# Sums of weight quarters in the first feed-forward product: additions on VectorE, or accumulating transfers issued by GpSimd

## The chip, the core and the metric

The kernel runs on one core of a Trainium2 chip. The metric is the device time of one execution in microseconds (us). Five engines run their own instruction streams in order and wait for one another through semaphores: TensorE (PE, matmuls), VectorE (DVE), ScalarE (ACT), GpSimd (POOL) and SyncE (SP, which here only issues transfers). Transfers (DMA) are carried by 16 DMA engines, whichever engine issued them.

## The reference

One layer of a hybrid encoder, in float32, for 512 tokens of width 2048: a mixer (a gated short convolution and a gated linear attention), its output projection, and a feed-forward block. The change lies in the first product of the feed-forward block, `h @ w_ff1[l]`, of 512 x 2048 by 2048 x 8192.

```python
x = x + y @ w_out[l]
h = rmsnorm(x, norm2_g[l])
x = x + jnp.square(jax.nn.relu(h @ w_ff1[l])) @ w_ff2[l]
return rmsnorm(x, norm_f_g)
```

## The kernel before

Matmuls run on float32 values that are split in two: "hi" is the value cast to the matmul's own float type (ACT), "lo" is the rest, value minus hi (DVE). A product of two such operands is three matmuls, hi by hi, hi by lo and lo by hi.

The first feed-forward product goes through 32 groups (`for g in range(NPAIR)`), each for 256 of the 8192 columns. In a group the product is done block by block with seven block products instead of eight, a scheme of Strassen's kind. The weight has four quarters of 128 x 1024 numbers (512 KB), b11, b12, b21 and b22; the activations stand ready in seven combinations, `hforms`, computed before the loop. The seven products, called forms here, need these weights:

| form | weight | output bank | remark |
|---|---|---|---|
| 1 | b12 | f1a | copied out as q1 before form 2 adds to the bank |
| 2 | b22 | f1a | onto form 1 |
| 5 | b11 + b12 | f1c | copied out as q5 before form 3 adds to the bank |
| 3 | b21 | f1c | onto form 5 |
| 7 | b11 + b21 | f1d | |
| 6 | b11 + b12 + b21 | f1b | |
| 4 | b11 + b12 + b21 + b22 | f1e | |

Each form is 24 matmuls of 256 columns (8 steps by three) and takes its weight through `split_w`: a cast on ACT into one of three "hi" buffers, a subtraction on DVE into one of three "lo" buffers. The three buffers go round in program order, so a cast waits until PE has ended the form three places earlier in that order. Before, the order is 1, 5, 7, 3, 6, 2, 4. The sums come from `plus`, a DVE addition of two 128 x 1024 tiles into one of three "w" buffers, four a group. At the end DVE and ACT combine the banks into the tile y, ACT squares it, and 512 KB go to DRAM (`a_keep`), to be read by the second feed-forward product.

The quarters are loaded by SP into four "raw" buffers, which belong to a pool (`wp`) that serves the whole kernel. The pool `f1`, with the w tiles, y, q1, q5, u and v, is opened for this loop; its memory is that of the residual tiles `xr`, which are stored to DRAM (`x_keep`) just ahead of the loop. PSUM has eight banks "fb", of which a group takes five.

The kernel's text is recorded and ordered anew by a scheduler: on an engine instructions need not stand in the order of the text, though the order is fixed once built. Names in the rows below: `raw_f_21`, `w_f_20` are group 2's tiles of quarter 1 and 0 as they stand in `w_ff1` (0 is b12, 1 is b11, 2 is b21, 3 is b22), `hi_f_83` is group 8's hi of form 3, a last number is a buffer's.

Of the kernel before, what the change touches and what calls it, by code (L numbers as in the profile page):

```python
# [29 lines left out]
UNIT = 1056  # L30
HALF = SEQ // 2
NPAIR = D_FF // (2 * P)
FORMS = (1, 5, 7, 3, 6, 2, 4)
RAWS = 4
# [5 lines left out]
def hymba_kernel(  # L40
# [3 lines left out]
    nc = tc.nc  # L44
    V, S, T, G = nc.vector, nc.scalar, nc.tensor, nc.gpsimd
# [3 lines left out]
    wp = ctx.enter_context(tc.tile_pool(name="wp", bufs=2))  # L49
# [81 lines left out]
    for t, s in ((g2t, g2), (cgt, conv_g), (cwt, conv_w)):  # L131
# [13 lines left out]
        out=later, in_=later, pattern=[[-1, P]], compare_op=ALU.is_gt, fill=0.0,  # L145
# [45 lines left out]
    with tc.tile_pool(name="mix", bufs=1) as mix:  # L191
# [153 lines left out]
        for k in range(8):  # L345
            b = feature_major(w_feat[HEADS + k], u, f"og{k}")
            t = mix.tile([P, SEQ], F32, name=f"ogt_{k}", tag=f"hs{k % 2}")
# [3 lines left out]
        for h in range(HEADS):  # L351
            b = feature_major(w_feat[h], u, f"q{h}")
            q = mix.tile([P, SEQ], F32, name=f"q_{h}", tag=f"q{h}")
            V.scalar_tensor_tensor(
                out=q, in0=b, scalar=float(DK) ** -0.5, in1=r1b, op0=ALU.mult, op1=ALU.mult
# [127 lines left out]
    a_keep = tc.dram_tile([NPAIR, P, 2 * SEQ], F32, name="a_keep")  # L483
# [102 lines left out]
    def fbank(name):  # L586
        return fb.tile([P, 512], F32, name=name, tag="fb", bufs=8)


    with tc.tile_pool(name="f1", bufs=1, reuse_waits="tile") as f1:  # L590
        for g in range(NPAIR):
            raws = []
            for q in range(4):
                raw = wp.tile([P, UNIT], F32, name=f"raw_f1_{g}{q}", tag="raw", bufs=RAWS)
                nc.sync.dma_start(raw[:, :1024], w_ff1[4 * g + q])
                raws.append(raw[:, :1024])
            b12, b11, b21, b22 = raws

            def split_w(f, src):
                hi = wp.tile([P, UNIT], F32R, name=f"hi_f1_{g}{f}", tag="hi", bufs=3)  # L600
                lo = wp.tile([P, UNIT], F32R, name=f"lo_f1_{g}{f}", tag="lo", bufs=3)
                S.copy(hi[:, :1024], src)  # L602
                V.tensor_tensor(out=lo[:, :1024], in0=src, in1=hi[:, :1024].bitcast(F32), op=ALU.subtract)  # L603
                return hi, lo

            def plus(f, in0, in1):
                w = f1.tile([P, 1024], F32, name=f"w_{g}{f}", tag="w", bufs=3)
                V.tensor_tensor(out=w, in0=in0, in1=in1, op=ALU.add)  # L608
                return w

            def product(f, w, dst, start):
                hi, lo = split_w(f, w)
                for p in range(8):
                    c = slice(p * P, (p + 1) * P)
                    sh, sl = hforms[p][f]
                    for m, (l, r) in enumerate(((hi, sh), (hi, sl), (lo, sh))):
                        T.matmul(  # L617
                            dst[:, :HALF], l[:, c], r, start=start and p == m == 0,
                            stop=p == 7 and m == 2, skip_group_check=True,
                        )  # L620

            def half(name, bufs=2):
                return f1.tile([P, HALF], F32, name=f"{name}_{g}", tag=name, bufs=bufs)

            ba, bc, bd, bb, be = (fbank(f"f1{k}_{g}") for k in "acdbe")
            y = f1.tile([P, 2, SEQ], F32, name=f"y_{g}", tag="y", bufs=2)
            t1, t2 = slice(0, HALF), slice(HALF, SEQ)
            product(1, b12, ba, True)
            q1 = half("q1")
            S.copy(q1, ba[:, :HALF])  # L630
            w1 = plus(5, b11, b12)
            product(5, w1, bc, True)
            q5 = half("q5")
            S.copy(q5, bc[:, :HALF])
            product(7, plus(7, b11, b21), bd, True)
            product(3, b21, bc, False)
            w3 = plus(6, w1, b21)
            product(6, w3, bb, True)
            u_ = half("u")
            V.tensor_tensor(out=u_, in0=bb[:, :HALF], in1=q1, op=ALU.subtract)  # L640
            v_ = half("v")
            V.tensor_tensor(out=v_, in0=bd[:, :HALF], in1=u_, op=ALU.add)
            V.tensor_tensor(out=y[:, 0, t1], in0=bc[:, :HALF], in1=u_, op=ALU.add)
            V.tensor_tensor(out=y[:, 0, t2], in0=q5, in1=v_, op=ALU.add)
            product(2, b22, ba, False)
            product(4, plus(4, w3, b22), be, True)
            S.activation(y[:, 1, t1], ba[:, :HALF], AF.Relu)
            V.tensor_tensor(out=y[:, 1, t2], in0=be[:, :HALF], in1=v_, op=ALU.subtract)
            S.activation(y[:, 0, :], y[:, 0, :], AF.Relu)
            S.activation(y[:, 1, t2], y[:, 1, t2], AF.Relu)  # L650
            S.activation(y, y, AF.Square)
            nc.gpsimd.dma_start(a_keep[g], y.rearrange("p a b -> p (a b)"))

# [13 lines left out]
    with tc.tile_pool(name="ff", bufs=1, reuse_waits="tile") as ff:  # L667
# [19 lines left out]
        for blk in range(4):  # L687
            a = []
# [5 lines left out]
            for n in range(4):  # L694
                bs = [fbank(f"f2_{blk}{n}{i}") for i in range(NT)]
                for j in range(nu):
                    h, l = unit(w_ff2[(blk * 4 + n) * 8 + j], 1024, f"f2_{blk}{n}{j}")
                    for i in range(NT):
                        t = slice(i * P, (i + 1) * P)
# [8 lines left out]
        w2 = {}  # L708
        for n in range(4):
            for j in (6, 7):  # L710
                raw = wp.tile([P, UNIT], F32, name=f"raw_e{n}{j}", tag="raw", bufs=RAWS)
# [4 lines left out]
        for i in range(NT):  # L716
            t = slice(i * P, (i + 1) * P)
            x3 = x3s[i]
            for n in range(4):
                b = fbank(f"e_{i}{n}")  # L720
# [14 lines left out]
            for n in range(2):  # L735
# [3 lines left out]
                out=x3[:, cs[3]], in0=x3[:, cs[3]], scalar=r3, in1=gft[:, cs[3]], op0=ALU.mult, op1=ALU.mult  # L739
# [65 lines left out]
```

## Time and profile before

| | |
|---|---|
| median of 3 runs | 2172.0 us (2170.23 to 2172.83) |
| the profiled execution | 2173.21 us, its span 2171.3 us |
| granted TensorE clock, mean | 0.995 |
| busy: PE, DVE, ACT, POOL | 2137.6, 1141.4, 763.8, 29.1 us |
| DMA | 263.24 MB, 121 GB/s on average |
| the edited loop, first matmul to last store issued | 787.6 to 1438.9 us |

The span is from the first to the last instruction on the core. The page lists groups of equal instructions by line, engine and operation with what they write and read ("hi_f<-w"), their count, their busy time and the mean of one, and the idle time ahead of them with what ended it. The chain of waits follows the work that ended last. A timeline row gives start, duration, engine, line, operation, and in brackets the idle time before it with its releaser. A DMA row gives the issuing queue, the count, the size of one, and the median time from issue to landing. In rows cut from a window the releaser after "<-" is what the engine waited for.

### The profile page before, as it was taken

The page shows a single profiled execution, that of the slowest core. Times are in us where ns is not written, and L with a number is a line of the kernel's source. Part 1 is how long each engine was busy: PE and PEld are TensorE (multiplying, and loading weights), DVE is VectorE, ACT ScalarE, POOL GpSimd, SP SyncE. Part 2 cuts the span into 40 slices and gives each one's busy share as a digit, 9 for nine tenths or more (in the row PEclk, how much of TensorE's full clock was granted, in tenths as well). Part 3 has the DMA queues.
Part 4 walks back from the last instruction along what each step waited for, and adds up shares of the span by engine and source line. Part 5 has one row for each costly group of instructions (what it writes and reads, how often), then busy time and mean ns, then how long its engine had stood idle before and what let it go on. Part 6 is the DMA issues. An engine that isn't in the chain of part 4 may idle for free.

```text
span 2171.3 us, 28976 instructions
## 1 busy us (share of the span) xinstructions
PE 2137.6 (98%) x12248; PEld 1863.1 (86%) x12248; DVE 1141.4 (53%) x1336; ACT 763.8 (35%) x980; POOL 29.1 (1%) x60
## 2 busy tenths in 40 slices
PE   8999999999999989999999999989999999999998
PEld 6988877777888889999999999977888888888886
DVE  4232236656754487777777777745243233322345
ACT  6242212222333345545554554533122122121133
POOL 0000000000000000000000000000000000000000
PEclk9999999999999999999999999999999999999999
DMA  7222222222242243444334334466243343222232
GB/s 290 84 87 97 92 79 92 78 78 78 88 174 88 92 151 127 136 131 136 133 127 136 131 133 135 137 230 216 97 156 108 96 134 128 90 96 97 97 117 78
DMA packets 71090, 263.24 MB, mean 121 GB/s; under 512 B 8037, under 2 KB 8085, under 8 KB 68784
## 3 DMA queue, kind: packets, MB, share of 16 engines
q1 hardware_dynamic: 64224, 230.85, 32.2%
q0 software_dynamic: 6736, 30.55, 3.5%
q8 instruction: 95, 1.56, 0.3%
q14 instruction: 35, 0.29, 0.0%
HBM read 236.20 MB, written 25.17 MB: 120 GB/s over the span
## 4 chain that ended last, share of the span: by engine, by line
PE 88%; issue 8%; DMA 3%; DVE 1%; ACT 1%; SPq 0%; POOL 0%; ACTq 0%; POOLq 0%
PE f L75 10%; PE f L76 10%; PE f L77 10%; PE f1c L617 8%; PE f1a L617 8%; PE f1b L617 4%; PE f1d L617 4%; PE f1e L617 4%; DMA a<-a_keep 2%; PE fm_ch L75 1%; PE fm_cc L75 1%; PE tm_v L75 1%; PE tm_v L76 1%; PE tm_v L77 1%; PE fm_og L77 1%
## 5 line engine op out<-in xcount | busy, mean ns | idle before, releaser
L71 DVE TENSOR_TENSOR lo_f<-raw_f,hi_f 128x1024 fp32r<-128x1024 f32 x120 | 146.8, 1224 | 342.7 <-ACT hi_f L70 342.7
L70 ACT CAST hi_f<-raw_f 128x1024 fp32r<-128x1024 f32 x120 | 125.8, 1049 | 412.7 <-PE f L77 408.8
L603 DVE TENSOR_TENSOR lo_f<-w,hi_f 128x1024 fp32r<-128x1024 f32 x128 | 156.8, 1225 | 114.0 <-ACT hi_f L602 113.1
L602 ACT CAST hi_f<-w 128x1024 fp32r<-128x1024 f32 x128 | 134.6, 1051 | 160.5 <-PE f1c L617 107.7
L617 PE MATMUL f1c<-Sh,hi_f 128*128 128x256 f32 x512 | 145.0, 283 | 6.2 <-ACT hi_f L602 6.2
L617 PE MATMUL f1c<-Sh,lo_f 128*128 128x256 f32 x512 | 145.0, 283 | 0.4 <-DVE lo_f L603 0.4
L617 PE MATMUL f1c<-Sl,hi_f 128*128 128x256 f32 x512 | 144.7, 283 | 0.0
L617 PE MATMUL f1a<-Sh,hi_f 128*128 128x256 f32 x512 | 144.2, 282 | 0.0
L617 PE MATMUL f1a<-Sh,lo_f 128*128 128x256 f32 x512 | 144.1, 282 | 0.0
L617 PE MATMUL f1a<-Sl,hi_f 128*128 128x256 f32 x512 | 144.0, 281 | 0.0
L602 ACT CAST hi_f<-raw_f 128x1024 fp32r<-128x1024 f32 x96 | 100.9, 1051 | 110.2 <-PE f1b L617 55.7
L603 DVE TENSOR_TENSOR lo_f<-raw_f,hi_f 128x1024 fp32r<-128x1024 f32 x96 | 117.2, 1221 | 12.4 <-ACT hi_f L602 12.3
L75 PE MATMUL tm_op<-hi_op,yh 128*128 128x512 f32 (+1 forms) x304 | 106.2, 349 | 0.0
L76 PE MATMUL tm_op<-lo_op,yh 128*128 128x512 f32 (+1 forms) x304 | 105.3, 346 | 0.0
L77 PE MATMUL tm_op<-hi_op,yl 128*128 128x512 f32 (+1 forms) x304 | 105.0, 345 | 0.0
L617 PEld LDWEIGHTS f1c<-Sh,hi_f 128*128 128x128 f32 x512 | 97.6, 191 | 6.4 <-ACT hi_f L602 6.4
L617 PEld LDWEIGHTS f1c<-Sh,lo_f 128*128 128x128 f32 x512 | 97.4, 190 | 0.7 <-DVE lo_f L603 0.7
L617 PEld LDWEIGHTS f1c<-Sl,hi_f 128*128 128x128 f32 x512 | 97.2, 190 | 0.0
L617 PEld LDWEIGHTS f1a<-Sh,hi_f 128*128 128x128 f32 x512 | 96.8, 189 | 0.0
L617 PEld LDWEIGHTS f1a<-Sh,lo_f 128*128 128x128 f32 x512 | 96.7, 189 | 0.0
L617 PEld LDWEIGHTS f1a<-Sl,hi_f 128*128 128x128 f32 x512 | 96.5, 188 | 0.0
L608 DVE TENSOR_TENSOR w<-raw_f,raw_f 128x1024 f32<-128x1024 f32 x64 | 78.4, 1225 | 27.1 <-DMA raw_f<-in_w_ff 25.6
(572 smaller groups left out, 5754.0 us busy)
## 6 DMA issues: line engine op xcount, KB each, us to landing
raw_f<-in_w_ff SPq DMA_DIRECT2D x248, 512.0 KB, 3.5
a_keep<-y POOLq DMA_DIRECT2D x32, 512.0 KB, 2.9
a<-a_keep SPq DMA_DIRECT2D x32, 512.0 KB, 3.4
raw_op<-in_w_out SPq DMA_DIRECT2D x22, 512.0 KB, 3.5
raw_og<-in_w_feat SPq DMA_DIRECT2D x16, 512.0 KB, 3.3
raw_cc<-in_w_feat SPq DMA_DIRECT2D x16, 512.0 KB, 3.4
raw_ch<-in_w_feat SPq DMA_DIRECT2D x16, 512.0 KB, 3.4
raw_cb<-in_w_feat SPq DMA_DIRECT2D x16, 512.0 KB, 3.4
```

Source lines behind the costliest of these rows:

```text
L70: S.copy(hi[:, c], raw[:, c])
L71: V.tensor_tensor(out=lo[:, c], in0=raw[:, c], in1=hi[:, c].bitcast(F32), op=ALU.subtract)
L75: T.matmul(dst, l[0], r[0], start=start, stop=False)
L76: T.matmul(dst, l[0], r[1], start=False, stop=False)
L77: T.matmul(dst, l[1], r[0], start=False, stop=stop)
L602: S.copy(hi[:, :1024], src)
L603: V.tensor_tensor(out=lo[:, :1024], in0=src, in1=hi[:, :1024].bitcast(F32), op=ALU.subtract)
L608: V.tensor_tensor(out=w, in0=in0, in1=in1, op=ALU.add)
L617: T.matmul(dst[:, :HALF], l[:, c], r, start=start and p == m == 0, stop=p == 7 and m == 2, skip_group_check=True,)
```

## The change

Additions on DVE are gone from the loop. `plus` is now a transfer issued by POOL with `accum_op=add`: it reads its source and adds it to the destination tile, in place. Two tiles are built so. "chain" (two buffers, tag "w") is loaded with b12 and used for form 1; then b11 is added to it straight from DRAM (form 5), then b21 (form 6), then b22 (form 4). "w2" (one buffer) is loaded with b11, and b21 is added (form 7). Only b22 and b21 go to raw buffers now; b11 is read from DRAM twice. The order of the forms in the text becomes 1, 2, 7, 5, 3, 6, 4. The store of y is issued by ACT instead of POOL.

```diff
+            def plus(dst, src):
+
+                G.dma_start(dst, src, accum_op=ALU.add)
-            def plus(f, in0, in1):
-                w = f1.tile([P, 1024], F32, name=f"w_{g}{f}", tag="w", bufs=3)
-                V.tensor_tensor(out=w, in0=in0, in1=in1, op=ALU.add)
-                return w
...
+            chain = load(0, "w", 2)
+            b22 = load(3, "raw", RAWS)
+            w2 = load(1, "w2", 1)
+            b21 = load(2, "raw", RAWS)
+            plus(w2, b21)
+            product(1, chain, ba, True)
-            product(1, b12, ba, True)
             q1 = half("q1")
             S.copy(q1, ba[:, :HALF])
-            w1 = plus(5, b11, b12)
-            product(5, w1, bc, True)
+            plus(chain, w_ff1[4 * g + 1])
+            product(2, b22, ba, False)
+            S.activation(y[:, 1, t1], ba[:, :HALF], AF.Relu)
+            product(7, w2, bd, True)
+            product(5, chain, bc, True)
             q5 = half("q5")
             S.copy(q5, bc[:, :HALF])
-            product(7, plus(7, b11, b21), bd, True)
+            plus(chain, b21)
             product(3, b21, bc, False)
-            w3 = plus(6, w1, b21)
-            product(6, w3, bb, True)
+            product(6, chain, bb, True)
+            plus(chain, b22)
...
-            product(2, b22, ba, False)
-            product(4, plus(4, w3, b22), be, True)
-            S.activation(y[:, 1, t1], ba[:, :HALF], AF.Relu)
+            product(4, chain, be, True)
...
-            nc.gpsimd.dma_start(a_keep[g], y.rearrange("p a b -> p (a b)"))
+            S.dma_start(a_keep[g], y.rearrange("p a b -> p (a b)"))
```

On PE, before, a group's forms stand in the order of the text, each whole; here is the seam between form 1 and form 5 of group 8.

```order
L617 MATMUL f1a_7573<-Sl_5629,hi_f_81_7579 128x256
L617 MATMUL f1a_7573<-Sh_5628,lo_f_81_7580 128x256
L617 MATMUL f1c_7574<-Sh_4470,hi_f_85_7611 128x256
L617 MATMUL f1c_7574<-Sl_4471,hi_f_85_7611 128x256
L617 MATMUL f1c_7574<-Sh_4470,lo_f_85_7612 128x256
```

Now PE runs 1, 7, one matmul of 5, 2, the other 23 of 5, four of 6, 3, the other 20 of 6, 4. This is the seam between form 7 and form 2 of group 8, on PE.

```order
L618 MATMUL f1d_7535<-Sl_5629,hi_f_87_7608 128x256
L618 MATMUL f1d_7535<-Sh_5628,lo_f_87_7609 128x256
L618 MATMUL f1c_7534<-Sh_4470,hi_f_85_7636 128x256
L618 MATMUL f1a_7533<-Sh_4478,hi_f_82_7579 128x256
L618 MATMUL f1a_7533<-Sl_4479,hi_f_82_7579 128x256
```

And this, also on PE, the seam where form 5 ends and form 3 begins.

```order
L618 MATMUL f1c_7534<-Sh_5628,lo_f_85_7637 128x256
L618 MATMUL f1b_7536<-Sh_4476,hi_f_86_7695 128x256
L618 MATMUL f1b_7536<-Sl_4477,hi_f_86_7695 128x256
L618 MATMUL f1b_7536<-Sh_4476,lo_f_86_7696 128x256
L618 MATMUL f1b_7536<-Sh_4476,hi_f_86_7695 128x256
L618 MATMUL f1c_7534<-Sh_4474,hi_f_83_7667 128x256
```

So form 2 moved from sixth place to between the first and second matmul of form 5, and hi and lo of form 6 are needed ahead of form 3.

On ACT, before, from cast 3 of group 14 to the first activation of its y (tile y_8982), with cast 1 of group 15 between.

```order
L602 CAST hi_f_143_9075<-raw_f_142_8973 128x1024
L630 COPY q_14_9011<-f1a_8977 128x256
L602 CAST hi_f_146_9105<-w_9103 128x1024
L634 COPY q_14_9043<-f1c_8978 128x256
L602 CAST hi_f_142_9139<-raw_f_143_8975 128x1024
L602 CAST hi_f_144_9169<-w_9167 128x1024
L602 CAST hi_f_151_9217<-raw_f_150_9203 128x1024
L649 ACTIVATE y_8982<-y_8982 128x512
```

On ACT, now, from the end of group 20 over group 21 to the first cast of group 22.

```order
L658 ACTIVATE y_10298<-y_10298 128x1024
L608 CAST hi_f_215_10626<-w_f_210_10529 128x1024
L659 DMA a_keep<-y_10298 128x1024
L636 COPY q_21_10566<-f1a_10523 128x256
L608 CAST hi_f_213_10657<-raw_f_212_10535 128x1024
L608 CAST hi_f_216_10685<-w_f_210_10529 128x1024
L639 ACTIVATE y_10528<-f1a_10523 128x256
L643 COPY q_21_10654<-f1c_10524 128x256
L608 CAST hi_f_214_10720<-w_f_210_10529 128x1024
L608 CAST hi_f_221_10768<-w_f_220_10759 128x1024
```

The store of the last group's y stands between cast 5 and the copy q1, cast 6 directly behind cast 3, and the next group's cast 1 directly behind cast 4.

On POOL, which had one store a group, four adds a group now stand like this; w_f_50 is the chain of group 5 and w_f_61 the w2 tile of group 6.

```order
L603 DMA w_f_40_6619<-raw_f_43_6621 128x1024
L603 DMA w_f_50_6849<-in_w_ff 128x1024
L603 DMA w_f_50_6849<-raw_f_52_6855 128x1024
L603 DMA w_f_61_7083<-raw_f_62_7085 128x1024
L603 DMA w_f_50_6849<-raw_f_53_6851 128x1024
```

The w2 add of the next group stands ahead of the last chain add of this one.

More of the change, by code (lines that the diff above doesn't have):

```diff
@@ L591, in hymba_kernel, with load @@
         for g in range(NPAIR):
[L592 to L597, printed above, removed]
+            def load(q, tag, bufs):
+                if tag == "raw":
+                    t = wp.tile([P, UNIT], F32, name=f"raw_f1_{g}{q}", tag="raw", bufs=RAWS)[:, :1024]
+                else:
+                    t = f1.tile([P, 1024], F32, name=f"w_f1_{g}{q}", tag=tag, bufs=bufs)
+                nc.sync.dma_start(t, w_ff1[4 * g + q])
+                return t
+            def plus(dst, src):
+                G.dma_start(dst, src, accum_op=ALU.add)
             def split_w(f, src):
```

## The prediction

> **What bounds the kernel now.** I read the page from the top: the span and the busy line, then busy time by stretch of the span, then what TensorE (PE) and ScalarE (ACT) waited for, then the timeline of one group of the first feed-forward product (the loop that the change edits), then the DMA rows.
>
> ```profile
> span 2171.3 us, 28976 instructions
> PE 2137.6 (98%) x12248; PEld 1863.1 (86%) x12248; DVE 1141.4 (53%) x1336; ACT 763.8 (35%) x980; POOL 29.1 (1%) x60
> L608 DVE TENSOR_TENSOR w<-raw_f,raw_f 128x1024 f32<-128x1024 f32 x64 | 78.4, 1225 | 27.1 <-DMA raw_f<-in_w_ff 25.6
> ```
>
> PE is busy 98% of the span. The third row is half of what the change removes: 64 of the 128 additions on DVE, 1.225 us each.
>
> ```profile
> core 0: us, PE busy (x) PEld busy (x) DVE busy (x) ACT busy (x) POOL busy (x), PEclk, DMA share, GB/s
> 840.00:1420.00 580.00, 580.00 (x4889) 580.00 (x4888) 436.79 (x465) 299.79 (x380) 15.95 (x30) 1.00 0.40 132
> 801.00:802.00 1.00, 1.00 (x7) 1.00 (x7) 1.00 (x2) 0.00 (x0) 0.00 (x0) 0.50 0.05 20
> ...
> PE f1c L617 <- ACT hi_f L602: 6.2, 1, 6.2
> ```
>
> From 840 to 1420 us, 29 of the 32 groups, PE has no idle time at all, at a granted clock of 1.00, while DVE is busy 437 of 580 us (75%). So DVE's additions set nothing there, and removing them can give nothing there. The one wait of PE that concerns this loop is 6.2 us at its start.
>
> ```profile
> 1000.10 0.28 PE L617 MATMUL f1c<-Sh,hi_f 128*128 128x256 f32 x1
> 1002.96 0.28 PE L617 MATMUL f1d<-Sh,hi_f 128*128 128x256 f32 x1
> ...
> 1000.18 1.05 ACT L602 CAST hi_f<-raw_f 128x1024 fp32r<-128x1024 f32 x1 [0.18 <-PE f1a L617]
> 1003.04 1.05 ACT L602 CAST hi_f<-w 128x1024 fp32r<-128x1024 f32 x1 [1.54 <-PE f1c L617]
> 1013.79 0.64 ACT L649 ACTIVATE y<-y 128x512 f32<-128x512 f32 x1 [1.15 <-DVE y L644]
> 1014.50 1.05 ACT L602 CAST hi_f<-w 128x1024 fp32r<-128x1024 f32 x1
> 1015.45 0.38 ACT L647 ACTIVATE y<-f1a 128x256 f32<-128x256 f32 x1
> 1017.33 1.05 ACT L602 CAST hi_f<-w 128x1024 fp32r<-128x1024 f32 x1 [1.50 <-PE f1e L617]
> 1018.43 0.42 ACT L650 ACTIVATE y<-y 128x256 f32<-128x256 f32 x1
> 1018.88 1.06 ACT L651 ACTIVATE y<-y 128x1024 f32<-128x1024 f32 x1
> 1020.13 1.05 ACT L602 CAST hi_f<-raw_f 128x1024 fp32r<-128x1024 f32 x1 [0.19 <-PE f1a L617]
> ...
> 1004.12 1.23 DVE L603 TENSOR_TENSOR lo_f<-w,hi_f 128x1024 fp32r<-128x1024 f32 x1 [1.63 <-ACT hi_f L602]
> 1011.07 1.22 DVE L608 TENSOR_TENSOR w<-w,raw_f 128x1024 f32<-128x1024 f32 x1
> 1012.21 0.42 DVE L640 TENSOR_TENSOR u<-f1b,q 128x256 f32<-128x256 f32 x1
> ...
> 1020.24 0.53 POOL L652 DMA_DIRECT2D a_keep<-y  x1 [19.42 <-ACT y L651]
> ```
>
> This is the clockwork. The same cast starts at 1000.18 and 1020.13: a group takes 19.95 us, one of its seven products 2.85 us (1000.10 to 1002.96), one matmul 0.119 us. A cast starts 0.08 us after the product that held its buffer ends (1002.96 to 1003.04). DVE's "lo" starts 1.08 us after the cast (1003.04 to 1004.12) and ends 2.31 us after it. Two ACT operations in a row start 0.95 us apart (1014.50, 1015.45), two of DVE 1.14 us (1011.07, 1012.21). From the end of ACT's square (1018.88 + 1.06) to POOL's DMA (1020.24) is 0.30 us.
>
> **The change, part by part.** *Removed:* four additions on DVE a group, 4 x 1.225 x 32 = 157 us of DVE. Worth 0: PE covers them. If PE began to wait for DVE, they would count.
>
> *Added:* four accumulating transfers a group on POOL. No row shows one, so I bound the time L from POOL's start to the data's landing.
>
> ```profile
> q1 hardware_dynamic: 16704, 60.82, 32.6%
> q0 software_dynamic: 4176, 15.21, 6.5%
> ...
> raw_f<-in_w_ff SPq DMA_DIRECT2D x116, 512.0 KB, 3.5
> a_keep<-y POOLq DMA_DIRECT2D x30, 512.0 KB, 2.9
> ...
> x_keep<-xr POOLq DMA_DIRECT2D x1, 1024.0 KB, 4.3
> ...
> x_keep<-xr POOLq DMA_DIRECT2D x4, 1024.0 KB, 8.0
> ```
>
> POOL's plain 512 KB store lands in 2.9 us; its engines work 6.5% of 580 us for 15.21 MB, that is 29 stores, 1.30 us each (a load: 32.6% for 116, 1.63 us). An add fetches two operands of 512 KB and writes one. Lower bound: the store, 2.9 (the second fetch hides). Upper bound: 1 MB in a queue of such, 8.0. Nearest is the 1 MB that POOL stored alone, 4.3, which agrees with 2.9 + 1.30 = 4.2. I take 4.3 for the last add of a group, which has no other transfer beside it; 4.7 for the second, which meets the activation store and the next group's w2 add (0.4 for part of 1.30); 5.2 for the first, whose source lies in HBM (3.5 against 2.9: 0.6) and which meets a weight load (0.3 of its 1.63).
>
> What a page says of this: the Trainium skill, "Collectives: The Full Stack", section "The bandwidth ceiling: the fold count and why AG ≠ RS ≠ AR", has it that an add inside the DMA engines costs nothing for the arithmetic but needs two source reads on one ring, and so runs at half a copy's speed. That speaks against this change. By it an add would be about 2 x 1.30 of engine time, the 4.2 above; by the store's row alone it would be 2.9, and the sum below would come to 2195. No run so far shows which holds.
>
> *The path of an add.* The sum is now built in place, so each add must wait until both cast and lo have read the old value, and the next cast waits for the add. I count from t = 0, the start of cast 4 (the last form of a group); a prime marks the next group, whose cast 1' follows on ACT at 0.95 and lo 1' on DVE at 1.08 + 1.14 = 2.22, ending at 3.45. Chain C: 3.75 + L1 + 0.1 to cast 5'; 2.31 + 0.30 + L2 + 0.1 to cast 6'; the same with L3 to cast 4'. The 0.1 after a landing is an estimate between 0 and the 0.30 of the hop above. C = 9.27 + L1 + L2 + L3 = 9.27 + 14.2 = 23.5 us a group, against 19.95.
>
> *Moved: product 2 to second place, and PE's order.* PE now runs 1, 7, one matmul of 5, 2, the rest of 5, four matmuls of 6, 3, the rest of 6, 4. Cast 3 takes the buffer of product 2, which now ends just ahead of 5, and cast 6 stands behind cast 3 on ACT. Floor A0, with adds that cost nothing: lo 4 ends at 2.31, the other 22 matmuls of 4 at 4.92, product 1 at 7.77, 7 at 10.62, one matmul, 2 at 13.59. Cast 3' 13.67, cast 6' 14.62, lo 3' 14.75, lo 6' 15.89 to 17.12. PE has 23 matmuls of 5 (to 16.32) and two of 6 (16.56), and its third of 6 needs lo 6': 0.56 us of waiting, whatever L is. So 20.5 us a group at the least, 32 x 0.56 = 18 us. Chain A, the last add behind that lo: 17.12 + 0.30 + 4.3 + 0.1 = 21.8. Chain B, through ACT: cast 7' waits for product 4 (5.0), then come three activations (1.10 + 0.71 + 0.45 + 1.06, the spacings above) to cast 5' at 8.3; two times 2.71 and L2, L3 give 13.7 + 9.0 = 22.7. C is the longest. In C, PE waits in two places, for lo 6 and for lo 4, 3.5 us together.
>
> *The activation store* goes from POOL to ACT, behind cast 5 and ahead of the copy q1. Its issue costs about what SyncE pays for such a transfer:
>
> ```profile
> L691 SPq DMA_DIRECT2D a<-a_keep x32: 319/326/423, 1438.8 to 1803.7; - x32
> ```
>
> 0.33 us on ACT. q1 is then done at 9.05 + 1.05 + 0.33 + 0.36 = 10.8 (a copy of this size is near the 0.38 row), when PE reaches product 2 (10.74). Cost 0.06, hidden behind C; without that cover 2 us over all groups. Behind it wait cast 3 and cast 6, which have until 16.5.
>
> *Queues.* On SP the w2 load waits for lo 7 (7.3 us in); behind it stand the raw loads of a group that starts 13 us later, so it costs 0. On POOL the next w2 add stands ahead of the last chain add; it is issued near 11 and the chain add only at 19. The DMA engines go from 0.40 x 20 = 8 us a group to about 8 + 4 x 2.6 = 18 of 23.5.
>
> *The start of the loop.*
>
> ```profile
> 786.67 1.58 POOL L573 DMA_DIRECT2D x_keep<-xr  x3 [0.80 <-DVE xr L555]
> 787.62 0.36 PE L617 MATMUL f1a<-Sh,hi_f 128*128 128x256 f32 x1
> 793.76 0.37 ACT L630 COPY q<-f1a 128x256 f32<-128x256 f32 x1 [0.42 <-DMA x_keep<-xr]
> 796.13 1.23 DVE L608 TENSOR_TENSOR w<-raw_f,raw_f 128x1024 f32<-128x1024 f32 x1 [0.37 <-DMA x_keep<-xr]
> 799.68 0.58 PE L617 MATMUL f1c<-Sh,lo_f 128*128 128x256 f32 x1 [0.40 <-DVE lo_f L603]
> ```
>
> The pool of the chain tiles lies where the residual tiles were, and is free only when their stores land (793.8 and 796.1). Before, product 1 read a raw tile that had long been loaded and ran at 787.62; PE got going again at 799.68 with 28 matmuls done. Now already product 1's weights wait: loads at 793.8 and 796.1, 3.5 us each; w2 at 799.6, its add 0.3 + 4.3 later, cast 7 done at 805.3, with 26 matmuls behind it. That is 6 us later.
>
> *Sum.* 32 x (23.5 - 19.95) = 114, plus 6: 120 us. The profiled execution took 2173.2 us, 1.2 above the median; on the median 2172.0 + 120 = 2292, rounded to 2290.
>
> **The rivals.** (1) Adds as short as a store, L = 2.9: C = 18.0, B = 19.5, A = 20.4, and the order alone decides with 20.5: 18 + 4.6 at the start = 2195. For it: the 2.9 row. Against it: the second fetch, the HBM source. (2) Adds near the upper bound: all at 8.0, C = 33.3, 427 + 10 = 2609; from 6.3 on it is over 2440. For it: the queued 8.0. PE would then wait over 3.4 us at one place and lose clock too: after its 6.2 us wait it ran at 0.50 (the 801 row). The Trainium skill, "TensorE: Matmul & The Clock Gate", section "What's actually happening", gives the gate a window of about 3.4 us; by that rule my two waits, 2.2 and 1.3, are too short to trip it, and the trace has no wait of that size to test it. (3) Faster: product 5 no longer waits for DVE's addition at the start of the loop. If PE's 6.2 us went and the loop kept its 19.95, the time would be 2166. It decides only if chain tiles could be loaded before 787 and the buffer of cast 3 were free 0.56 us sooner; the 793.76 row and the order speak against both. (4) No change within 0.2% (4.3 us, about what the measurement can tell): the same with the start unchanged.
>
> **How the numbers follow.** The add chain sets the pace, L between 3.4 and 6.3 on average: 0.70, own range 2205 to 2440 (A at L = 3.4 is 20.9: 2172 + 31 + 5; C at 6.3 is 28.2: 263 + 8). Rival 1: 0.12. Rival 2: 0.12. Rival 3: 0.03. Unchanged: 0.03. The likeliest gives 2290. The range 2193 to 2440 takes in rival 1 and leaves out 0.18. Slower 0.94, same 0.03, faster 0.03.
>
> **What the changed profile would show.** Groups 23.5 us apart, not 20.5; PE waiting for lo_f and hi_f twice a group, 3 to 4 us in all; ACT's hi casts of the w tile waiting for DMA; adds landing in 4 to 5.5 us; the first matmul of the loop near 798 instead of 787.6; additions gone from DVE, POOL still almost idle. Rows of 2.9 us for adds, or waits on PE's own buffers only, would show rival 1; PEclk below 1.00 in the loop, rival 2. I am wrong in the direction if the loop stays at 19.95: then the buffer rule for cast 3 is not what the order says.

## The result, and the profile after

The changed kernel takes 2344.27 us (median of 4 runs, 2341.17 to 2345.64). The kernel before took 2172.41 us beside it (2170.23 to 2173.94). The ratio is 1.079, 95% interval 1.0771 to 1.0809: 172 us slower, where 118 were forecast on the median.

First the page: span, busy time, the casts of the w tiles, and the adds (count, size of one, median us from issue to landing).

```profile
span 2342.6 us, 29119 instructions
PE 2203.7 (94%) x12248; PEld 1902.1 (81%) x12248; DVE 982.2 (42%) x1208; ACT 749.0 (32%) x980; POOL 124.8 (5%) x156
L608 ACT CAST hi_f<-w_f 128x1024 fp32r<-128x1024 f32 x160 | 164.6, 1047 | 487.0 <-DMA w_f<-raw_f 311.4
w_f<-raw_f POOLq DMA_DIRECT2D x96, 512.0 KB, 4.8
w_f<-in_w_ff POOLq DMA_DIRECT2D x32, 512.0 KB, 6.2
```

Before, the casts of the w tiles stood so:

```profile
L602 ACT CAST hi_f<-w 128x1024 fp32r<-128x1024 f32 x128 | 134.6, 1051 | 160.5 <-PE f1c L617 107.7 <-PE f1e L617 46.8 <-DVE w L608 2.2
```

DVE lost its 157 us of additions (its busy time fell from 1141.4 to 982.2), and no time came back for them. Instead ACT stood still for 487.0 us ahead of the casts of the w tiles, 311.4 of it until an add from SBUF had landed; before, these casts waited for PE. The adds land in 4.8 us from SBUF and in 6.2 from DRAM (medians).

The windowed view of the loop (busy time of PE, weight loads, DVE, ACT, POOL; granted clock; share of the DMA engines; GB/s) answers to the row of before for the same 580 us:

```profile
core 0: us, PE busy (x) PEld busy (x) DVE busy (x) ACT busy (x) POOL busy (x), PEclk, DMA share, GB/s
840.00:1420.00 580.00, 507.44 (x3866) 487.25 (x3866) 231.92 (x277) 227.26 (x302) 80.96 (x92) 0.96 0.76 189
```

PE was busy in all 580 us before and is now in 507; the matmuls done fall from 4889 to 3866 and the clock from 1.00 to 0.96. The DMA share rose from 0.40 to 0.76. What PE waited for (us in total, times, the longest):

```profile
PE f1b L618 <- ACT hi_f L608: 42.2, 31, 2.7
PE f1b L618 <- DVE lo_f L609: 23.8, 32, 0.8
...
PE f1e L618 <- DVE lo_f L609: 12.2, 17, 0.8
PE f1c L618 <- ACT hi_f L608: 9.5, 16, 1.4
PE f1e L618 <- ACT hi_f L608: 6.1, 11, 1.2
```

These recur in the groups: at form 6 (bank f1b), form 4 (f1e) and form 5 (f1c), the three forms that take the chain tile after an add. They sum to 93.8 us, 2.9 a group.

The timeline of one group on ACT, DVE and POOL shows the cycle, from one cast 4 to the next:

```profile
1097.80 2.00 ACT L608 CAST hi_f<-w_f 128x1024 fp32r<-128x1024 f32 x2 [5.53 <-DMA w_f<-raw_f]
1108.21 1.05 ACT L608 CAST hi_f<-w_f 128x1024 fp32r<-128x1024 f32 x1 [2.18 <-DMA w_f<-in_w_ff]
1115.39 1.04 ACT L608 CAST hi_f<-w_f 128x1024 fp32r<-128x1024 f32 x1 [4.91 <-DMA w_f<-raw_f]
1122.64 2.00 ACT L608 CAST hi_f<-w_f 128x1024 fp32r<-128x1024 f32 x2 [5.66 <-DMA w_f<-raw_f]
1098.88 2.36 DVE L609 TENSOR_TENSOR lo_f<-w_f,hi_f 128x1024 fp32r<-128x1024 f32 x2 [5.90 <-ACT hi_f L608]
...
1101.53 0.88 POOL L603 DMA_DIRECT2D w_f<-in_w_ff  x1 [7.38 <-DVE lo_f L609]
1110.81 1.77 POOL L603 DMA_DIRECT2D w_f<-raw_f  x2 [8.40 <-DVE lo_f L609]
1117.99 0.90 POOL L603 DMA_DIRECT2D w_f<-raw_f  x1 [5.41 <-DVE lo_f L609]
```

Cast 4 and cast 1' start at 1097.80, lo 1' ends at 1101.24, the first add is issued at 1101.53 and cast 5' starts at 1108.21. Cast, lo, POOL, landing, next cast: that repeats for form 6 (1110.81 to 1115.39) and form 4 (1117.99 to 1122.64). The pieces are 3.73 + 6.68 + 2.60 + 4.58 + 2.60 + 4.65 = 24.84 us, the whole distance of the two casts 4. There is no piece of PE in it, and each cast's releaser is a DMA. The other groups are like it: of these three casts in the 31 groups behind the first, 92 of 93 start 0.08 us after their add has landed.

Last, the copy q1, once a group, gives the beat.

```profile
L636 ACT COPY q<-f1a x32: 360/365/369, 805.3 to 1584.6; 128x256 f32<-128x256 f32 x32
```

The first q1 comes 11.6 us later (805.33 against 793.76). The first gap from one q1 to the next is 27.9 us in both. The other 30 gaps average 25.05 against 19.94, 153.1 us. What follows the last q1 grew by 6.7. That is the 171.3 us by which the spans differ (2342.6 and 2171.3).

### The profile page after: what moved, and what is told of

It reads as the page before. It is cut to its first block, busy times and chain, and to the rows that moved or that the text cites. A ratio compares the mean times of both kernels' runs of the same rounds, so it can differ in the third digit from the quotient of the medians.

```text
span 2342.6 us, 29119 instructions
## 1 busy us (share of the span) xinstructions
PE 2203.7 (94%) x12248; PEld 1902.1 (81%) x12248; DVE 982.2 (42%) x1208; ACT 749.0 (32%) x980; POOL 124.8 (5%) x156
## 5 line engine op out<-in xcount | busy, mean ns | idle before, releaser
L609 DVE TENSOR_TENSOR lo_f<-w_f,hi_f 128x1024 fp32r<-128x1024 f32 x160 | 193.3, 1224 | 485.1 <-ACT hi_f L608 468.4
L608 ACT CAST hi_f<-w_f 128x1024 fp32r<-128x1024 f32 x160 | 164.6, 1047 | 487.0 <-DMA w_f<-raw_f 311.4
L71 DVE TENSOR_TENSOR lo_f<-raw_f,hi_f 128x1024 fp32r<-128x1024 f32 x120 | 146.7, 1224 | 340.7 <-ACT hi_f L70 340.7
L70 ACT CAST hi_f<-raw_f 128x1024 fp32r<-128x1024 f32 x120 | 125.6, 1049 | 410.7 <-PE f L77 408.5
L618 PE MATMUL f1c<-Sh,hi_f 128*128 128x256 f32 x512 | 160.2, 313 | 9.9 <-ACT hi_f L608 9.5
L618 PEld LDWEIGHTS f1c<-Sh,hi_f 128*128 128x128 f32 x512 | 110.5, 216 | 15.0 <-ACT hi_f L608 14.7
L618 PE MATMUL f1b<-Sh,hi_f 128*128 128x256 f32 x256 | 77.0, 301 | 42.2 <-ACT hi_f L608 42.2
L618 PEld LDWEIGHTS f1c<-Sl,hi_f 128*128 128x128 f32 x512 | 110.4, 216 | 0.0
L603 POOL DMA_DIRECT2D w_f<-raw_f x96 | 84.4, 984 | 456.6 <-DVE lo_f L609 433.8
L618 PE MATMUL f1b<-Sh,lo_f 128*128 128x256 f32 x256 | 76.9, 300 | 23.8 <-DVE lo_f L609 23.8
```

The costliest lines, as they stand in the source:

```text
L70: S.copy(hi[:, c], raw[:, c])
L71: V.tensor_tensor(out=lo[:, c], in0=raw[:, c], in1=hi[:, c].bitcast(F32), op=ALU.subtract)
L603: G.dma_start(dst, src, accum_op=ALU.add)
L618: T.matmul(dst[:, :HALF], l[:, c], r, start=start and p == m == 0, stop=p == 7 and m == 2, skip_group_check=True,)
```

## The experiments

The theory was that the in-place chain sets the beat: cast, lo and add of one tile follow one another three times a group. Its rivals were the new order of the forms alone, the traffic of the DMA engines, and the clock. Ratios are to the kernel before, run on the same chip (2172.8 to 2173.3 us there). Diffs are against the changed kernel unless said otherwise.

### Same order, sums on DVE (e1)

```diff
-                G.dma_start(dst, src, accum_op=ALU.add)
+                V.tensor_tensor(out=dst, in0=dst, in1=src, op=ALU.add)
...
+            b11 = f1.tile([P, 1024], F32, name=f"b11_{g}", tag="b11", bufs=1)
+            nc.sync.dma_start(b11, w_ff1[4 * g + 1])
...
-            plus(chain, w_ff1[4 * g + 1])
+            plus(chain, b11)
```

> The changed kernel in every order (forms, PE's seams, buffers), but the four sums of a group are made in place by DVE additions instead of transfers; b11 gets a tile of its own. Theory (the chain of adds sets the pace, C = 9.0 + L1 + L2 + L3): with additions of 1.2 us the chain is about 13 us and only the order's floor A0 of 20.5 us a group is left: 32 x 0.56 = 18 us and about 3 at the start, 2193 us. Rival 1 (the new order itself is what costs 5 us a group): stays above 2300. Rival 2 (there is no floor): 2175.

Measured 2189.64 us, ratio 1.0075 (1.0059 to 1.0092). Its loop:

```profile
850.00:1400.00 550.00, 550.00 (x4568) 544.82 (x4567) 404.63 (x436) 272.60 (x352) 0.00 (x0) 1.00 0.48 157
```

PE has no idle time that the view counts, and the copies q1 stand 20.25 us apart. So the order and the buffers cost 0.30 us a group (9 us in all) and the start some 7. Of the 172 us, 155 vanish when DVE adds instead. In-place sums as such are not the fault; the way they are added is.

### The same transfers as plain copies (e2)

This kernel leaves the sums out: the transfer overwrites its destination. Every wait and order stays.

```diff
-                G.dma_start(dst, src, accum_op=ALU.add)
+                G.dma_start(dst, src)
```

> The changed kernel with the same transfers at the same places, but plain copies: they overwrite the tile instead of adding to it, so the sums are left out. Theory: a copy lands in about 3.0 us (3.6 from HBM), chain C about 19, so the floor of 20.5 to 20.7 decides: 2195 to 2205 us, and the adds' extra time over a copy is what the change costs. Rival (it is the transfer as such, its issue and receipt, and not the second fetch): copies land in 4.5 or more and the time stays above 2290.

Measured 2206.71 us, ratio 1.0156 (1.0136 to 1.0176). That is just above the 2195 to 2205 us expected, and far from the rival's 2290. Its loop (850 to 1400 us): POOL's queue (packets, MB, share of the 16 engines) and the landings.

```profile
q0 software_dynamic: 15353, 55.88, 27.3%
w_f<-raw_f POOLq DMA_DIRECT2D x79, 512.0 KB, 3.3
w_f<-in_w_ff POOLq DMA_DIRECT2D x26, 512.0 KB, 4.7
```

And the queue in the changed kernel, 850 to 1550 us:

```profile
q0 software_dynamic: 16128, 58.73, 46.7%
```

A copy lands in 3.3 and 4.7 us, an add in 4.8 and 6.3 (in the loop). The first of each pair, from SBUF, is a median over two kinds of transfer. Those that the chain waits for land in 2.9 us as copies and in 4.6 as adds; the one for w2, which POOL issues right behind the second chain transfer, lands in 3.7 and 6.8. A copy takes 27.3% of 550 us for 105 transfers, 1.43 us of all 16 engines; an add 46.7% of 700 us for 112, 2.92 us: 2.04 times as much. POOL's issue takes 0.53 us for a copy (528 ns on average) and 0.87 for an add. So the staircase from 2172 is: the order 2190, a copy's landing time in the chain 2207, the add in place of the copy 2344.

The Trainium skill ("Collectives: The Full Stack", "The bandwidth ceiling: the fold count and why AG ≠ RS ≠ AR") says that an add reads two sources on one ring and so runs at half a copy's speed; the 2.04 agrees with it.

### All adds into one scratch tile (e3)

The sums are left out: each add goes to a tile that no form reads.

```diff
+        scr = f1.tile([P, 1024], F32, name="scr", tag="scr", bufs=1)
+        V.memset(scr, 0.0)
...
-                G.dma_start(dst, src, accum_op=ALU.add)
+                G.dma_start(scr, src, accum_op=ALU.add)
```

> The changed kernel with all 128 accumulating transfers, but added into a scratch tile that nobody reads: the sums are left out, and no cast waits for a transfer of POOL. The traffic of the adds stays. Theory (the waits for the adds cost, not their traffic): floor of 20.5 us, about 2193 us. Rival (the load on the DMA engines slows the weight loads and the rest): above 2250.

Measured 2377.72 us, ratio 1.0943 (1.0921 to 1.0965), far from it. POOL's rows in one group tell why:

```profile
1101.34 0.87 POOL L605 DMA_DIRECT2D scr<-raw_f  x1 [5.02 <-DMA scr<-in_w_ff]
1106.11 0.87 POOL L605 DMA_DIRECT2D scr<-raw_f  x1 [3.90 <-DMA scr<-raw_f]
```

One scratch tile makes a chain of its own: each add waits for the landing of the one before, so that these two stand 4.8 us apart, and the groups 26.1. The experiment moved the chain instead of removing it and decides nothing; e9 below repeats it with four tiles.

### First add from SBUF (e4)

```diff
+            b11 = f1.tile([P, 1024], F32, name=f"b11_{g}", tag="b11", bufs=1)
+            nc.sync.dma_start(b11, w_ff1[4 * g + 1])
...
-            plus(chain, w_ff1[4 * g + 1])
+            plus(chain, b11)
```

> The changed kernel, but b11 is loaded into a tile of its own ahead of time, and the first chain add takes it from there instead of from HBM. Theory: the first add lands like the others, 4.8 instead of 6.3 us, and the chain is 1.5 us a group shorter: 48 us less, 2296 us. Rival (the first add is long because it meets the weight loads, wherever its source lies): within 10 us of 2344.

Measured 2378.24 us, ratio 1.0947 (1.0931 to 1.0963): slower than the changed kernel, against the expectation. Landings in its loop, and the second add of one group with the cast that waits for it:

```profile
w_f<-raw_f POOLq DMA_DIRECT2D x79, 512.0 KB, 5.2
...
w_f<-b POOLq DMA_DIRECT2D x27, 512.0 KB, 4.9
```
```profile
1122.21 0.87 POOL L603 DMA_DIRECT2D w_f<-raw_f  x1 [6.99 <-DVE lo_f L609]
1128.89 1.04 ACT L608 CAST hi_f<-w_f 128x1024 fp32r<-128x1024 f32 x1 [5.40 <-DMA w_f<-raw_f]
```

The first add did fall, from 6.3 to 4.9. But b11 now needs a load of its own, which SP issues just ahead of w2's load, and the second add then takes 6.68 us instead of 4.58; groups are 26.3 us apart. In this group the gain of 1.4 us on one add came back as 2.1 on the next; on average the first add got 1.3 us shorter and the second 2.3 longer. So the time of an add depends on what else the engines carry, and a price from one place does not hold at another.

### Only form 7's sum as an add (e5)

Against the kernel before; only w2 is built by a transfer. The quarter b11 is loaded a second time for it, and the "w" buffers of the DVE sums go from three to two.

```diff
+            w2 = f1.tile([P, 1024], F32, name=f"w2_{g}", tag="w2", bufs=1)
+            nc.sync.dma_start(w2, w_ff1[4 * g + 1])
+            G.dma_start(w2, b21, accum_op=ALU.add)
...
-            product(7, plus(7, b11, b21), bd, True)
+            product(7, w2, bd, True)
```

> The kernel before, with one of its four additions a group as an accumulating transfer: b11 + b21 for form 7, which stands outside the chain and is needed a group later than it could be issued. Theory (a transfer that nobody waits for costs nothing): within 4 us of 2172. Rival (accumulating transfers cost by being there): slower by 10 us or more.

Measured 2177.91 us, ratio 1.002 (1.0011 to 1.0029): 4.6 us more, a little over what the theory allowed.

```profile
850.00:1400.00 550.00, 550.00 (x4636) 550.00 (x4635) 384.58 (x416) 282.89 (x357) 39.47 (x55) 1.00 0.62 185
w<-raw_f POOLq DMA_DIRECT2D x28, 512.0 KB, 7.1
```

This add takes 7.1 us, longer than the 4.8 and 6.2 of the changed kernel, and PE has no idle time: groups stay 19.95 apart. Nobody waits for it, since w2 has a tile of its own and can be built a group ahead. The 4.6 us lie in the first group, whose gap is 34.0 us instead of 27.9. So an add of this length cost the loop nothing; it has no place in the chain.

### A fourth buffer for form 2 (e6)

```diff
+                x = f in (2,)
+                hi = (f1 if x else wp).tile([P, 1024 if x else UNIT], F32R, name=f"hi_f1_{g}{f}", tag="hx" if x else "hi", bufs=1 if x else 3)
...
```

> The changed kernel with a fourth pair of hi and lo buffers, used by form 2 alone, so that cast 3 no longer waits for product 2. Theory (the chain of adds is longer than the floor and hides it): within 8 us of 2344. Rival (the buffer wait of cast 3 is part of the loss): 15 to 20 us less.

Measured 2408.7 us, ratio 1.1082 (1.1067 to 1.1097). The scheduler gave the forms another order: on PE form 2 now comes after five matmuls of form 7. It needs the copy q1 that much sooner, and on ACT q1 still stands behind cast 5, so PE waits for q1 in each group:

```profile
PE f1a L619 <- ACT q L637: 113.7, 31, 4.6
```

This is another kernel than the one meant, and the run doesn't test the buffer.

### Form 1 of the next group ahead of form 4 (e7)

The loads, form 1 and the first add of group g+1 are written ahead of form 4 of group g, so that the first add need not wait for cast 4.

```diff
+        nxt = head(0)
         for g in range(NPAIR):
+            chain, b22, w2, b21, ba, q1 = nxt
...
+            if g + 1 < NPAIR:
+                nxt = head(g + 1)
-            product(4, chain, be, True)
+            product(g, 4, chain, be, True)
```

> The changed kernel with the text's order turned so that the next group's form 1, its cast and its first add come ahead of form 4 of this group: same adds, same traffic, but the first add of one group runs beside the last add of the group before. Theory (one group's adds are chained to the next group's only through ACT's order): the loop falls to PE's pace or the floor, 20.0 to 21 us a group, 2180 to 2215 us. Rival (the DMA engines are the limit: about 19 us of work a group): no better than 2290.

Measured 2262.04 us, ratio 1.0406 (1.0392 to 1.042): about half of the loss is gone without making any add shorter and with the DMA engines busier than in the changed kernel (0.85 of the loop against 0.76), as the chain theory has it and a theory of traffic does not. It did not reach the expectation. POOL and ACT in one group:

```profile
1117.77 1.05 ACT L605 CAST hi_f<-w_f 128x1024 fp32r<-128x1024 f32 x1 [0.56 <-PE f1e L611]
1120.37 0.87 POOL L600 DMA_DIRECT2D w_f<-raw_f  x1 [11.75 <-DVE lo_f L606]
1121.68 0.87 POOL L600 DMA_DIRECT2D w_f<-raw_f  x1 [0.44 <-issue]
1127.32 1.99 ACT L605 CAST hi_f<-w_f 128x1024 fp32r<-128x1024 f32 x2 [5.04 <-DMA w_f<-raw_f]
```

Cast 5 now waits for the buffer of product 4, which waits for the add of form 4; and the second add, issued 1.31 us ahead of the w2 add, takes 6.95 us. The period is 22.46 us on average. The group shown is one of the slower ones: 22 of the 31 gaps are 21.2 to 22.1 us, and seven, this one among them, 24.1 to 24.8.

### A better start for the kernel before (e8)

Against the kernel before; only group 0 differs. Form 5's sum goes into the raw tile, q1 into a pool that is free early, and forms 2 and 3 come ahead of form 7.

```diff
+                w = in1 if g == 0 and f == 5 else f1.tile([P, 1024], F32, name=f"w_{g}{f}", tag="w", bufs=3)
...
+                pool, tag = (wp, "first") if g == 0 and name == "q1" else (f1, name)
+                return pool.tile([P, HALF], F32, name=f"{name}_{g}", tag=tag, bufs=1 if pool is wp else bufs)
...
-            product(7, plus(7, b11, b21), bd, True)
+            if g > 0:
+                product(7, plus(7, b11, b21), bd, True)
+            else:
+                product(2, b22, ba, False)
...
```

> The kernel before with DVE additions; only its first group is changed: form 5's sum is made in place in a raw tile, q1 lies in another pool, and forms 2 and 3 come ahead of form 7, so that PE needs nothing from the memory of the residual tiles until four forms are done. Theory (the wait for the stores of the residual at the start of the loop is on PE's path in both kernels): 6.2 + 0.8 + 0.4 us of waiting and 1.3 us of half clock behind it fall away, 6 to 9 us less than before, 2164 us. Rival (something else is late there next, such as the last h forms): less than 3 us gained.

Measured 2164.4 us (2162.8 to 2166.07), ratio 0.9958 (0.9945 to 0.9972): 0.4% faster than the kernel before. The longest wait of PE that is left at the start is 0.40 us, for a cast. The wait of 6.2 us that the prediction's third rival spoke of was real and worth having; no add by transfer is needed for it.

### Four scratch tiles (e9)

The sums are left out: each of a group's four adds has its own scratch tile.

```diff
+        scrs = [f1.tile([P, 1024], F32, name=f"scr{n}", tag=f"scr{n}", bufs=1) for n in range(4)]
...
-                G.dma_start(dst, src, accum_op=ALU.add)
+                turn[0] += 1
+                G.dma_start(scrs[turn[0] - 1], src, accum_op=ALU.add)
```

> As the run with one scratch tile (the sums are left out, all 128 accumulating transfers stay), but each of a group's four adds has a scratch tile of its own, so that no add waits for the add before it. Theory (it is waiting for adds that costs, and the one scratch tile made the adds a chain again): no cast waits for POOL, 20.2 to 21 us a group, 2190 to 2215 us. Rival (about 18 us of work a group for the DMA engines delays the weight loads themselves): above 2250.

Measured 2254.75 us, ratio 1.0375 (1.0354 to 1.0396), between the two expectations. Two stretches, and from the first a cast, and what SP waited for between 850 and 1050 us (us in total, times, the longest):

```profile
900.00:1000.00 100.00, 76.16 (x590) 74.00 (x589) 35.31 (x41) 34.48 (x45) 21.66 (x25) 0.88 0.93 206
```
```profile
1050.00:1400.00 350.00, 347.22 (x2863) 343.75 (x2864) 175.24 (x205) 172.78 (x226) 47.43 (x54) 0.99 0.84 217
```
```profile
947.21 1.04 ACT L613 CAST hi_f<-w_f 128x1024 fp32r<-128x1024 f32 x1 [16.02 <-DMA w_f<-in_w_ff]
```
```profile
SPq L602 <- DMA scr<-raw_f: 166.0, 13, 20.3
```

With only their scratch tile to wait for, the adds from DRAM ran ahead of their groups. While they did, the DMA engines were at 0.93, and four groups (917 to 1055 us) took 32 to 38 us, in each of which a cast waited 13 to 18 us for a weight load. The load itself was not what took so long. The cast of 947.21 waits for a load that SP issued at 940.51 and that landed 6.6 us later; in the second stretch such loads take 5.4. SP issued it late, because it stood behind a raw load whose buffer an add was still reading until 940.01. That add had been held up on POOL by adds from DRAM, which follow one another in their one scratch tile (issued at 926.22 and 932.05). The other three are alike, but for the last, whose load also took 11.4 us. So most of this loss is once more a queue in which transfers that were not urgent held up one that was, and not the fullness of the engines.

From 1050 us on, with three adds a group still moving and the engines at 0.84, groups stand 20.22 us apart, as in e1 (PE takes eleven matmuls of form 6 ahead of form 3 here instead of four). So there the adds that nobody waits for cost nothing.

### The first chain add on DVE (e10)

```diff
-            plus(chain, w_ff1[4 * g + 1])
+            V.tensor_tensor(out=chain, in0=chain, in1=b11, op=ALU.add)
```

(b11 is loaded as in e4.)

> The changed kernel with only the first chain add (b11, for form 5) back on DVE, from a tile of its own; orders on PE and ACT as in the changed kernel but for one copy. Theory: that add leaves the chain, but cast 5 still stands behind product 4 and three activations (8.3 us after cast 4), so chain B decides: 13.7 + 4.7 + 4.8 = 23.2 us a group against 24.8, about 50 us less than the changed kernel, 2285 to 2295 us. Rival (each add costs its full time): 24.8 - 5 = about 20 us a group, 2185.

Measured 2303.84 us, ratio 1.0601 (1.0583 to 1.0618), some 9 us above the expectation. The adds left land in 5.0 us and the period is 23.8. Two casts of one group, 7' and 5':

```profile
1108.91 1.06 ACT L608 CAST hi_f<-w_f 128x1024 fp32r<-128x1024 f32 x1 [2.22 <-PE f1e L618]
1111.80 1.03 ACT L608 CAST hi_f<-w_f 128x1024 fp32r<-128x1024 f32 x1
```

By the prediction's chain B, 13.7 + 2 x 5.0 = 23.7. That chain runs through product 4 on PE, cast 7' and the three activations on ACT to cast 5', which here starts without idle time 8.06 us after cast 4 (8.3 forecast). It takes over when the first add is gone: 6.3 us of add are worth only 1.3 us a group.

### The last chain add on DVE (e11)

```diff
-            plus(chain, b22)
+            V.tensor_tensor(out=chain, in0=chain, in1=b22, op=ALU.add)
```

> The changed kernel with only the last chain add (b22, for form 4) back on DVE. Theory (chain C): the chain loses about 4.8 us and gains a DVE addition of 1.2: 3.75 + 6.2 + 2.6 + 4.7 + 2.3 + 1.3 = 20.9 us a group, 2205 to 2220 us. Rival (the load on the DMA engines sets the pace, one add of four less): about 2300.

Measured 2403.84 us, ratio 1.106 (1.1044 to 1.1077): one add fewer, and 60 us slower than the changed kernel. Rows of DVE, POOL and ACT in one group:

```profile
1104.86 1.23 DVE L609 TENSOR_TENSOR lo_f<-w_f,hi_f 128x1024 fp32r<-128x1024 f32 x1 [1.98 <-ACT hi_f L608]
1108.07 1.77 POOL L603 DMA_DIRECT2D w_f<-raw_f  x2 [9.67 <-DMA w_f<-in_w_ff]
1115.22 1.04 ACT L608 CAST hi_f<-w_f 128x1024 fp32r<-128x1024 f32 x1 [6.11 <-DMA w_f<-raw_f]
```

The scheduler's order changed with the edit: on PE form 2 now lies inside form 7, and on POOL the next group's w2 add stands ahead of the second chain add. It waits for the w2 load, which SP issued at 1102.90. The chain add, whose lo ended at 1106.09, is issued behind it near 1108.95, and cast 6 starts at 1115.22: 8.8 us after the chain add could have gone (1106.39) instead of 4.7. About 2.6 of the 4.1 lie ahead of the issue, the rest in a longer landing beside the w2 add. POOL issues in order, and a transfer that was not urgent held up one that was.

### Only the w2 sum on DVE (e12)

```diff
-            plus(w2, b21)
+            V.tensor_tensor(out=w2, in0=w2, in1=b21, op=ALU.add)
```

> The changed kernel with only the sum for form 7 (w2) back on DVE; the three chain adds stay. Theory: the w2 add stands outside the chain, but it runs right behind the second chain add on the same DMA engines; without it the chain keeps its form and its adds may land some tenths sooner: 2300 to 2345 us. Rival (all four adds cost alike): about 40 us less, 2300 or below.

Measured 2334.77 us, ratio 1.0743 (1.0727 to 1.0759); period 24.7.

```profile
w_f<-raw_f POOLq DMA_DIRECT2D x44, 512.0 KB, 4.6
w_f<-in_w_ff POOLq DMA_DIRECT2D x23, 512.0 KB, 5.5
```

With the w2 add gone the first chain add lands sooner (5.5 us instead of 6.3). The other two do not: 4.6 is also what they take in the changed kernel, where the 4.8 counts w2's adds too. Nearly the whole loss stays with three adds a group. The scheduler moved form 2 inside form 7 here as well, so the 10 us gained cannot be put down to one cause. Together with e5: the add off the chain is almost free, the three on it make the loss.

## Why the prediction was right, and where it was off

**The chain.** The path that the prediction called C is the one that sets the beat; the row-by-row sum above is its formula. What it had as 9.27 beside the adds measures 8.93 in the group shown and 9.00 on average over the last 30 groups, with the hops counted to the adds (9.27 less three of 0.1 is 8.97). The mis-sized terms are the adds: with their hops 5.3, 4.8 and 4.4 were forecast, 14.5 together; they average 6.39, 4.79 and 4.81, together 16.0. So it is mostly the first, L1: the 0.6 for its source in DRAM came from a load against a store (3.5 and 2.9), and e4, where its source moved to SBUF, made that add 1.3 us shorter. The second came out as forecast. The last, taken without other transfers beside it, was 0.4 short. The engine time of an add was forecast at 2.6 and is 2.92. The period came out 1.55 us above the 23.5 forecast, 47 of the 52 us missed; the start (11.6 against 6 + 3.55) and the end (6.7 against 3.55) make up the other 5.

**DVE's additions** were worth 0, as said: before they were covered by PE, and after by the adds. e1, with the additions back and the order kept, runs without idle PE in the windowed view.

**The order of the forms.** The floor was put at 20.5 us, 0.56 of waiting a group; e1 and the second part of e9 measure 20.25 and 20.22, about 0.30. The mechanism given for it was wrong. "Cast 3 takes the buffer of product 2" does not hold; in the changed order casts 3 and 6 don't follow the rule, told with the kernel, that a cast waits for the form three places earlier. Cast 3, the copy q5 and the first matmul of form 3 in one group of e1:

```profile
1134.16 1.05 ACT L608 CAST hi_f<-raw_f 128x1024 fp32r<-128x1024 f32 x1 [1.51 <-PE f1d L618]
1140.01 0.37 ACT L645 COPY q<-f1c 128x256 f32<-128x256 f32 x1 [1.53 <-PE f1c L618]
1140.44 0.39 PE L618 MATMUL f1c<-Sh,hi_f 128*128 128x256 f32 x1
```

Cast 3 waits for product 7 (bank f1d) and starts at 1134.16, when the first matmul of product 2 (1134.20) has not begun; it is so in the groups of the changed kernel too. It is cast 6 that waits for product 2. So lo of form 6 is early enough. What PE loses lies at the first matmul of form 3, which adds to the bank f1c. In each of 27 groups of e1 it starts 0.05 us after the copy q5 of that bank has ended, and from the matmul before it to the one behind it pass 0.49 us instead of the 0.24 of two steps. That the floor came out near its forecast was luck, and the error did no harm only because C is longer. For the same reason e6 had nothing to gain: in the groups read cast 3 never waits for product 2.

**Chains A and B** were rightly put below C. B showed itself in e10, at 23.8 where its formula gives 23.7. A was not isolated.

**The start.** The first matmul of the loop belongs to the step that was said to be 6 us later:

```profile
798.80 0.58 PE L618 MATMUL f1a<-Sh,hi_f 128*128 128x256 f32 x1 [12.88 <-ACT hi_f L608]
```

It was forecast near 798, and cast 7 was to be done at 805.3; product 7 starts at 805.47.

**Queues and the store.** The store on ACT never shows as the releaser of a wait in the groups read. POOL's issue was taken to be like its store's, 0.53; it is 0.87, but POOL still idles most of the loop. The order on POOL that was costed at nothing did cost nothing here, because w2's load came in time; e11 is the case in which it did not.

**The clock.** That "my two waits, 2.2 and 1.3, are too short to trip it" was wrong. PE's matmuls at form 6 of the quoted group, and two windows around them:

```profile
1116.49 0.39 PE L618 MATMUL f1b<-Sh,hi_f 128*128 128x256 f32 x1 [1.03 <-ACT hi_f L608]
1117.75 0.58 PE L618 MATMUL f1b<-Sh,lo_f 128*128 128x256 f32 x1 [0.75 <-DVE lo_f L609]
```
```profile
1114.33:1117.74 3.41, 1.64 (x12) 1.23 (x10) 1.23 (x1) 1.59 (x3) 0.00 (x0) 1.00 1.01 195
1117.74:1121.15 3.41, 3.40 (x16) 3.40 (x17) 0.00 (x0) 0.00 (x0) 0.90 (x1) 0.50 0.89 240
```

Waits of 1.03 and 0.75 us, with matmuls between them, were enough: the clock is 0.50 from 1117.74 to 1121.15, 3.41 us, and 1.00 on both sides. The Trainium skill ("TensorE: Matmul & The Clock Gate", "What's actually happening") speaks of an idle window of about 3.4 us; this trace has no idle stretch of that length in the group, and the clock halved. What the trace shows instead is a grid. All half-speed stretches of this loop begin whole multiples of 3.41 us from one another, and what goes with them is how little PE was busy in the step before: 1.64 of 3.41 us here. From 830 to 1500 us 15 steps at full clock were followed by half clock, with PE busy for at most 0.48 of each; those followed by full clock had 0.54 or more, but for one with 0.48. So several short waits within one step did here what the prediction expected of one long wait only.

"PEclk below 1.00 in the loop" was to be a sign of rival 2; it came with C. PE's busy time rose by 66 us (2203.7 - 2137.6), 2.1 us a group, of which the clock explains 1.0 (0.96 against 1.00 over 25 us); the rest was not told apart. With the 2.9 of waiting (3.5 were forecast, at forms 6 and 4 alone) that is 5.0, the group's growth from 19.95 to 25.05. But that sum is a second account of the same time, not a second cause: the chain holds no work of PE, so a faster PE would have waited longer; no run tests that.

**The rivals.** Adds as short as a store were refuted by the 4.6 to 6.4 us of the chain's adds, and what they would have given (2195) is near what e2 measured with true copies (2207). Adds near 8 us did not happen on the chain. Nor was the direction in doubt: the first matmul of the loop came 11 us later and the loop didn't hold its 19.95. (The buffer rule for cast 3 was indeed not as said, which was named as a sign of a wrong direction; the chain of adds kept the loop slow all the same.)

## What to carry to other kernels

Before an operation is moved from an engine with slack to the DMA engines, write down the chain of reads and writes of its buffer: in place, each add must wait for the last reader and the next reader for the landing, and here a path of three such adds, with the casts and subtractions between them, was the whole beat (24.84 of 24.84 us in the group shown) while one add off the chain, at 7.1 us, cost nothing in the loop. Take an accumulating transfer at twice a copy's engine time, as measured here, and expect its landing to move with whatever else is loading. When a step is taken off the chain, look for the next chain and for the place of the remaining transfers in their queue: of five attempts to relieve this one (e4, e7, e10, e11, e12) three gained 10 to 82 us and two lost.

## What the runs showed of the hardware that was not expected

- An accumulating transfer of 512 KB from SBUF lands in 4.6 us on the chain where a copy takes 2.9, from DRAM in 6.3 where a copy takes 4.7, and in 6.8 right behind another add; it takes the 16 engines 2.92 us against 1.43, and POOL 0.87 us to issue against 0.53.
- The TensorE clock fell to half for 3.41 us after two waits of 1.03 and 0.75 us. In this loop it goes by steps of 3.41 us, and a step in which PE was busy for less than about half (at most 0.48) was followed, but for one, by a step at half clock.
- A transfer that waits holds up the later ones of the engine that issues it: on POOL an add on the chain by about 2.6 us (e11), and through POOL and SP the weight loads, for which casts then waited 13 to 18 us (e9).

What stays open: whether the kernel keeps 20.25 us a group with all four adds taken off the chain and none of them running ahead, and the part of PE's longer busy time that the clock does not explain.
